# A hybrid attention and HGRN2 block on one core: one more page slot, another block order, and whole rows in the merge

## The chip, the cores and the metric

The kernel runs on 1 core of one Trainium2 chip. The metric is the device time of one execution in microseconds. The engines are named as the profile names them: PE (TensorE), PEld (its weight loads), DVE (VectorE), ACT (ScalarE), POOL (GpSimd) and SP (SyncE, which issues most DMAs). A difference of 0.3% is about what a measurement of this kernel can tell from no change.

## The reference

One layer on 1024 tokens of 1024 features. One input projection `z = rms_norm(x) @ w_in` feeds two branches, everything in float32:

```
q, k, v = qkv of 3 groups x 8 heads of 64;  (window, dilation) = (128,1), (512,4), (2048,16)
o_g = softmax(rms_norm(q) . rms_norm(k) / 8 + bias, in the band) @ v         # per group g
wts = den_g * exp(max_g - max over g)
o_a = sum_g wts_g * o_g / sum_g wts_g                                          # the merge
y_a = (o_a * silu(g_a)) @ w_proj_a
f   = lb + (1 - lb) * sigmoid(z_f);  S_t = diag(f_t) S_(t-1) + (1 - f_t) i_t^T;  o_t = S_t^T q_t
o_b = rms_norm(o_fwd + o_bwd) * silu(g_b);  y_b = o_b @ w_proj_b               # 8 heads, both directions
out = x + (sigmoid(zgate_a) * y_a + sigmoid(zgate_b) * y_b) @ w_out
```

Group g's outputs lie in DRAM by residue classes of its dilation (1, 4 or 16), so a token's three outputs stand at three places of a row.

## The kernel before

**Products in two parts.** Each float32 operand is kept as a high and a low part of type fp32r. A product is three matmuls (high·high, low·high, high·low). The weights come in *pages* of 128x512: loaded into `raw` (or `qraw`), turned into `whi` by ACT, and into `wlo = raw - whi` by DVE or POOL (`split`, line 381). While `b.low` is "dma", `wlo` is made otherwise: ACT writes −`whi` into it, and POOL issues a DMA that adds the page from DRAM. Two rings of RING slots hold the split pages; a slot comes free when PE has used its page (`free_to`).

**Who sets the order.** All instructions are issued by a planner in program order of Python, with an estimate of each engine's time. PE's main stream (projection units, blocks) is written out; between its pieces `tick` (line 274) issues the tasks of the other engines that are due, and `burst` (line 290) the small PE products that are ready. So a change of a ring's size or of an order in one place moves instructions in many. Each engine works through its own list in order. All instructions carry line 60, that of the recording helper, and are told apart by their tiles.

**The stages, in time.**
- 0 to 58 us: h is prepared, and the products `u` of the first value group (pages 0 to 7) run twice over, for the two halves of the tokens (`u_products`, line 985). During the second loop the pages 8 to 15 are split, with `b.low = "dma"`.
- 55 to 148 us: `v` of groups 1 and 2. Tiles `gp`; each sweep reads eight pages, 8 to 15 and then 16 to 23. The first sums `xs` of h for the next stage are made in it.
- 148 to 676 us: 27 *blocks* of seven products each, by Strassen's scheme (`start_quads`, line 413; `run_quads`, line 477). A product is 12 matmuls with one page, and the page is a sum or difference of quarters of the block's weights; these wait in a ring of QRAW tiles of 512 KB, two for each block. The list `blocks` (lines 698 to 701) sets their order: qk (q and k of the attention, with a norm chain of squares, `nss` sums, logarithm and exponential behind each), sg (gates), qb (q of the second branch), gb and ga (gates with silu). Results leave PSUM as `qA`, `qC`, `qE` through `stage` and `spare`.
- 692 to 860 us: the attention, 860 to 921 us: the merge, mixed with the projections of the first HGRN heads.
- 906 to 1234 us: the HGRN heads, 1234 us to the end: the last projections by the seven-product scheme.

**The merge.** `alphas_out` (line 1648) makes the weights of the groups, `alB`. For each of 8 units (four pairs of heads, two halves of the tokens) `merge_load` (line 1649) loads the three group outputs `og` and the gate `gal`, and `spread_al` (line 1684) spreads the weights by three matmuls into three PSUM banks `al`, then multiplies and adds on DVE into `macc`. In halves of a row, group 1's loads have runs of 512 bytes, group 2's of 128 bytes.

**The first HGRN head.** Its transposes `kT` on PE need `sk`, which DVE makes at the end of a chain that begins with the scans `Bc`. On DVE these stand behind the last unit of the merge.

Of the kernel before, what the change touches and what calls it, by code (L numbers as in the profile page):

```python
# [9 lines left out]
F32R = mybir.dt.float32r  # L10
# [3 lines left out]
OP = mybir.AluOpType  # L14
# [4 lines left out]
S = 1024  # L19
# [2 lines left out]
NEG = -1e30  # L22
TABW = 384
WARM = 10
RING = 8
RAWS = 4
LEAD = 4
TAIL, LATE = 4, 4
EARLY = 8
QB = 6  # L30
QRAW, SPARE = 4, 7
RES = (1, 4, 16)
LOWS = ("T2", "T4")
SQ, EA = 2, 6
# [198 lines left out]
class Builder:  # L233
# [179 lines left out]
    def start_quads(self, ring):  # L413
# [238 lines left out]
def hybrid_block(ctx, tc, a, out):  # L652
    b = Builder(ctx, tc, a)
    a_, v_, g_, t_, s_ = b.p.act, b.p.dve, b.p.pool, b.p.pe, b.p.sp
# [19 lines left out]
    def bank(name):  # L674
        t = b.bank.get(name=name)
        b.bank.done(t)
        return t
# [18 lines left out]
    qk = [("qk", g, hv, e) for g in range(3) for hv in range(2) for e in range(2)]  # L696
    sg = [("sg", 0, j) for j in range(0, 8, 2)] + [("sg", 1, j) for j in range(0, TAIL, 2)]
    blocks = []
    for k in range(6):
        blocks += qk[2 * k:2 * k + 1] + sg[k:k + 1] + qk[2 * k + 1:2 * k + 2] + ([("qb", 2 * k - 2)] if 0 < k <= QB // 2 else [])  # L700
    blocks += [("gb", k) for k in range(4)] + [("ga", 0), ("ga", 2)]

    def block_pages(kind, *at):
# [25 lines left out]
    items += [wpa[i] for i in range(8)]  # L729
    b.setup_weights(items, wpool, RING, RAWS)  # L730

# [45 lines left out]
    acc = [v_ring.get() for _ in range(2)]  # L777
# [259 lines left out]
    for j in range(4):  # L1037
        keep_u(j)
    b.low = "dma"
    at = {0: {11: lambda: root(1)}, 3: {5: lambda: root_out(1), 11: lambda: root(0)}, 7: {5: lambda: root_out(0)}}  # L1040
    for d in range(8):
        u_products(1, d, at.get(d, {}))
# [196 lines left out]
    def scaled(g, hv, e, half, z, y2, o, col, count):  # L1239
        R = RES[g]  # L1240
        n = 512 // R
        per = lambda t: t.rearrange("p (r u) -> p r u", r=R) if R > 1 else t
        nat = lambda t: t.rearrange("p (u r) -> p r u", r=R) if R > 1 else t
        v_.tensor_tensor(per(o), nat(y2), nat(z), op=OP.mult)
# [5 lines left out]
        def out():  # L1250
            for i in range(4):
# [333 lines left out]
    mer = {}  # L1585

    def merge_maybe(now=False):
        if mer or not (now or len(stored) == 48) or not att:
            return
        if now:  # L1590
            b.drain()
        b.eager, b.SLACK = False, 0.6
        b.low = "dve"
        psum(3)
        actx.close()
        mer["p"] = mctx.enter_context(tc.tile_pool(name="merge", bufs=1, side="right"))
        mer["sel"] = sel = mer["p"].tile([128, 3, 4, 128], F32R, name="sel")
        mer["x"] = mer["p"].tile([128, 8, 128], F32R, name="mx")
        g_.memset(mer["x"].bitcast(F32), 0.0)
        pick = lambda c: ident[:, c:c + 8].rearrange("p (a j) -> p a j", a=4)[:, :, :, None].to_broadcast([128, 4, 2, 64])  # L1600
        for g in range(3):
            v_.tensor_tensor(sel[:, g].rearrange("p a (j c) -> p a j c", j=2), pick(32 * g), pick(32 * g + 8), op=OP.add)
        mer["og"] = b.ring(mer["p"], "og", 9, [128, 512])
        mer["gal"] = b.ring(mer["p"], "gal", 3, [128, 512])
        mer["acc"] = b.ring(mer["p"], "macc", 2, [128, 512])
        merge_start()

# [38 lines left out]
        b.product(0, [mer["x"]], alphas_out, merge=False, banks=2)  # L1646

    def alphas_out():
        ab = mer["p"].tile([128, S], F32R, name="alB")
        for half in range(2):  # L1650
            p = bank("alT")
            for t in range(4):
                t_.transpose(p[:, 128 * t:128 * t + 128], mer["x"][:, 4 * half + t].bitcast(F32), ident)
            a_.activation(ab[:, 512 * half:512 * half + 512], p, AF.Copy)
        mer["ab"] = ab

    def merge_load(p, half):
        ld = {}

        def og_load(g):  # L1660
            o = mer["og"].get()
            if g == 0:
                s_.dma_start(o, oD[0, p, :, 512 * half:512 * half + 512])
            else:
                R = 4 if g == 1 else 16
                U = S // R
                s_.dma_start(o.rearrange("p (r u) -> p r u", r=R),
                             oD[g, p].rearrange("p (r u) -> p r u", r=R)[:, :, U // 2 * half:U // 2 * half + U // 2])
            ld[g] = o

        def ga_load():
            t = mer["gal"].get()
            s_.dma_start(t, gaD[p, half])
            ld[3] = t

        for g in range(3):
            b.task("sp", [oD], lambda g=g: og_load(g), 1, lambda: mer["og"].soon())
        b.task("sp", [gaD], ga_load, 1, lambda: mer["gal"].soon())
        b.product(4, [], lambda: spread_al(p, half, ld),
                  lambda: len(ld) == 4 and "ab" in mer and b.p.done(mer["ab"]) <= b.p.t["pe"]  # L1680
                  and b.when_all(list(ld.values())) and mer["acc"].soon(),
                  merge=False, banks=3)

    def spread_al(p, half, ld):
# [4 lines left out]
        per = lambda t, g: t.rearrange("p (r u) -> p u r", r=(4, 16)[g - 1])  # L1689
        acc = mer["acc"].get()  # L1690
# [12 lines left out]
    def merge_start():  # L1703
        mer["st"] = st = mer["p"].tile([128, 3, 2, 8, 8], F32, name="nst")
        stats_in()
        a_.activation(st[:, 0], mst[0], AF.Copy)
        b.task("dve", [st], alphas, 3)
        for k in range(8):
            merge_load(k // 2, k % 2)


    def evac_sg(w, j, half):
# [471 lines left out]
    ep, acc, sgr = ectx["ep"], ectx["acc"], ectx["sg"]  # L2184
# [30 lines left out]
    def seven_weights(base, pages, order, along=None, by_dma=()):  # L2215
# [13 lines left out]
        def split(op, i):  # L2229
# [3 lines left out]
            def f():  # L2233
# [346 lines left out]
```

## Time and profile before

| | |
|---|---|
| three runs | 1437.22, 1433.92, 1433.57 us; median 1433.92 |
| profiled execution | 1435.38 us, of which the span of the trace is 1433.6 |
| mean granted clock of PE | 0.995 |
| busy: PE, DVE, ACT, POOL | 1408.3, 918.0, 848.3, 349.5 us |
| DMA | 230.31 MB, mean 161 GB/s |

The span is counted from the first to the last instruction of the profiled execution; times in the text are from its start. A row of a timeline gives the start, the duration, engine, operation, tiles (out<-in) and how many instructions it stands for; in brackets the idle time before it and what ended that. Matmuls overlap: one of 128x512 lasts 0.39 us, and the next can start before it ends. A row of the waits gives what an engine waited for, the total, the number of waits and the longest.

### The profile page before, as it was taken

What the parts mean: (1) busy time and instruction counts of PE and PEld (TensorE: products, weight loads), DVE (VectorE), ACT (ScalarE), POOL (GpSimd) and SP (SyncE); (2) the same over time, 40 slices, a digit from 0 to 9 for tenths busy, and PEclk for the clock granted to TensorE, in tenths of its full rate; (3) what the DMA queues carried; (4) which work ended last, traced back from release to release, by engine and by line L of the source; (5) the groups of instructions that cost most, each with busy time, mean ns of one, the idle gap of its engine ahead of it and who ended that gap; (6) DMA issues with size and microseconds to landing.
All of it is one profiled execution on the core that took longest, in us unless ns stands there. A gap on an engine that the chain in (4) does not pass through costs nothing. (4 is left out here: it accounts for less than half of the span.)

```text
span 1433.6 us, 24071 instructions
## 1 busy us (share of the span) xinstructions
PE 1408.3 (98%) x8506; PEld 1170.7 (82%) x8506; DVE 918.0 (64%) x1890; ACT 848.3 (59%) x1837; POOL 349.5 (24%) x378
## 2 busy tenths in 40 slices
PE   9999999999999999999999999899999999999998
PEld 8778888888888888788778888688888888788887
DVE  6574556666666666542356647978878686358973
ACT  7642656655555565843586642667777684558461
POOL 0100434454433333243141110122123121001011
PEclk9999999999999999999999999999999999999999
DMA  6737566677744434533887239745445443768565
GB/s 225 176 105 212 163 204 160 150 182 174 169 131 118 103 89 98 158 112 117 286 282 254 94 85 273 209 109 126 103 118 126 123 131 87 236 231 220 176 170 143
DMA packets 200804, 230.31 MB, mean 161 GB/s; under 512 B 60531, under 2 KB 125323, under 8 KB 200172
## 3 DMA queue, kind: packets, MB, share of 16 engines
q1 hardware_dynamic: 182876, 193.19, 44.4%
q0 software_dynamic: 16944, 35.40, 13.2%
q8 instruction: 67, 1.10, 0.3%
q14 instruction: 53, 0.43, 0.1%
q10 hardware_dynamic: 864, 0.19, 0.1%
HBM read 168.77 MB, written 81.43 MB: 175 GB/s over the span
## 5 line engine op out<-in xcount | busy, mean ns | idle before, releaser
L60 POOL TENSOR_TENSOR wlo<-qraw,whi 128x512 fp32r<-128x512 f32 x135 | 181.2, 1344 | 390.5 <-ACT whi L60 383.8
L60 ACT ACTIVATE whi<-qraw 128x512 fp32r<-128x512 f32 x189 | 117.7, 626 | 101.6 <-POOL wlo L60 36.8
L60 PE MATMUL gp<-hh,whi 128*128 128x512 f32 x264 | 109.0, 413 | 0.0
L60 DVE TENSOR_TENSOR qraw<-qraw,qraw 128x512 f32<-128x512 f32 x81 | 70.0, 865 | 57.6 <-POOL wlo L60 57.6
L60 PE MATMUL gp<-hh,wlo 128*128 128x512 f32 x264 | 103.6, 392 | 0.0
L60 PE MATMUL gp<-hl,whi 128*128 128x512 f32 x264 | 103.0, 390 | 0.0
L60 ACT ACTIVATE whi<-raw 128x512 fp32r<-128x512 f32 x92 | 57.5, 626 | 75.8 <-DMA raw<-in_w_in_dram 38.3
L60 ACT ACTIVATE as<-as,neg 128x192 f32<-128x192 f32 (+1 forms) x192 | 77.8, 409 | 23.9 <-DVE neg L60 23.9
L60 PE MATMUL qA<-hh,whi 128*128 128x512 f32 x216 | 84.0, 389 | 0.0
L60 PE MATMUL qA<-hl,whi 128*128 128x512 f32 x216 | 84.0, 389 | 0.0
L60 PE MATMUL qA<-hh,wlo 128*128 128x512 f32 x216 | 84.0, 389 | 0.0
L60 PE MATMUL gp<-wlo,hh 128*128 128x512 f32 x192 | 76.0, 396 | 4.0 <-DMA wlo<-in_w_in_dram 3.0
L60 PE MATMUL gp<-whi,hh 128*128 128x512 f32 x192 | 79.6, 415 | 0.0
L60 PE MATMUL gp<-whi,hl 128*128 128x512 f32 x192 | 75.8, 395 | 0.0
L60 POOL COPY mm<-Bc 128x8 f32<-128x8 f32 x64 | 32.5, 543 | 171.6 <-DVE Bc L60 171.6
L60 POOL DMA_DIRECT2D wlo<-in_w_in_dram x36 | 31.1, 864 | 142.1 <-ACT wlo L60 92.3
L60 DVE CUSTOM_DVE_ANT_0 as<-sc,abias 128x192 f32<-128x192 f32 (+1 forms) x192 | 48.4, 308 | 21.3 <-PE sc L60 12.4
L60 PEld LDWEIGHTS gp<-hh,wlo 128*128 128x128 f32 x264 | 49.5, 188 | 10.9
L60 PEld LDWEIGHTS gp<-hh,whi 128*128 128x128 f32 x264 | 49.7, 188 | 8.9
L60 PEld LDWEIGHTS gp<-hl,whi 128*128 128x128 f32 x264 | 49.8, 189 | 8.3
L60 DVE TENSOR_TENSOR wlo<-qraw,whi 128x512 fp32r<-128x512 f32 x54 | 38.4, 711 | 28.2 <-ACT whi L60 28.1
L60 DVE TENSOR_TENSOR ny<-ny,spare 128x512 f32<-128x512 f32 x36 | 55.7, 1549 | 0.0
(316 smaller groups left out, 4123.5 us busy)
## 6 DMA issues: line engine op xcount, KB each, us to landing
raw<-in_w_in_dram SPq DMA_DIRECT2D x84, 256.0 KB, 3.1
qraw<-in_w_in_dram SPq DMA_DIRECT2D x60, 256.0 KB, 4.3
qraw<-in_w_in_dram SPq DMA_DIRECT2D x24, 512.0 KB, 4.4
qkD<-ny SPq DMA_DIRECT2D x192, 64.0 KB, 2.1
wlo<-in_w_in_dram POOLq DMA_DIRECT2D x36, 256.0 KB, 4.4
sg<-sgD SPq DMA_DIRECT2D x32, 256.0 KB, 3.7
eraw<-wsD SPq DMA_DIRECT2D x32, 256.0 KB, 3.1
sgD<-stage SPq DMA_DIRECT2D x26, 256.0 KB, 2.2
```

Of the source, the lines that this page charges most:

```text
L60: got = f(*args, **kw)
```

## The change

The change has three parts:
- RING goes from 8 to 9 slots and QRAW from 4 to 3 tiles, which needs as much memory as before. One more page is split ahead of the second loop of `u_products`.
- The blocks are ordered anew: one qb block goes between the qk blocks, the other two behind all of them and ahead of gb and ga. Before, the three were spread between the qk blocks.
- The merge loads whole rows of a group's output, 12 loads of 512 KB in the order of groups 2, 1, 0, in a ring of 6 tiles of 1024 columns; before, 24 loads of 256 KB in a ring of 9 tiles of 512. The gates' ring goes from 3 to 2, `alB` is written into the tile `mx`, and the product of group 2 is written into its PSUM bank in place of an `og` tile. The rows come free after the second half.

```diff
-RING = 8
+RING = 9
...
-QRAW, SPARE = 4, 7
+QRAW, SPARE = 3, 7
...
-        blocks += qk[2 * k:2 * k + 1] + sg[k:k + 1] + qk[2 * k + 1:2 * k + 2] + ([("qb", 2 * k - 2)] if 0 < k <= QB // 2 else [])
+        blocks += qk[2 * k:2 * k + 1] + sg[k:k + 1] + qk[2 * k + 1:2 * k + 2] + ([("qb", 0)] if k == 2 else [])
+    blocks += [("qb", h) for h in range(2, QB, 2)]
     blocks += [("gb", k) for k in range(4)] + [("ga", 0), ("ga", 2)]
...
     b.low = "dma"
+    b.split_next_page()
     at = {0: {11: lambda: root(1)}, 3: {5: lambda: root_out(1), 11: lambda: root(0)}, 7: {5: lambda: root_out(0)}}
...
-        mer["og"] = b.ring(mer["p"], "og", 9, [128, 512])
-        mer["gal"] = b.ring(mer["p"], "gal", 3, [128, 512])
+        mer["og"] = b.ring(mer["p"], "og", 6, [128, S])
+        mer["gal"] = b.ring(mer["p"], "gal", 2, [128, 512])
...
-        ab = mer["p"].tile([128, S], F32R, name="alB")
+        ab = mer["x"].rearrange("p t h -> p (t h)")
...
+        def og_load(g):
+            rows[g] = mer["og"].get()
+            s_.dma_start(rows[g], oD[g, p])
...
-        for g in range(3):
+        for g in (2, 1, 0):
             b.task("sp", [oD], lambda g=g: og_load(g), 1, lambda: mer["og"].soon())
...
-        v_.tensor_tensor(ld[0], al[0], ld[0], op=OP.mult)
-        v_.tensor_tensor(nat(acc, 1), nat(al[1], 1), per(ld[1], 1), op=OP.mult)
-        v_.tensor_tensor(nat(ld[1], 2), nat(al[2], 2), per(ld[2], 2), op=OP.mult)
-        v_.tensor_tensor(ld[0], ld[0], ld[1], op=OP.add)
-        v_.tensor_tensor(acc, acc, ld[0], op=OP.add)
-        v_.tensor_tensor(acc, acc, ld[3], op=OP.mult)
+        acc, far = mer["acc"].get(), al[2]
+        near = rows[0][:, 512 * half:512 * half + 512]
+        v_.tensor_tensor(near, al[0], near, op=OP.mult)
+        v_.tensor_tensor(nat(acc, 1), nat(al[1], 1), per(1), op=OP.mult)
+        v_.tensor_tensor(nat(far, 2), nat(al[2], 2), per(2), op=OP.mult)
+        v_.tensor_tensor(near, near, far, op=OP.add)
+        v_.tensor_tensor(acc, acc, near, op=OP.add)
+        v_.tensor_tensor(acc, acc, gate, op=OP.mult)
...
-        for g in range(3):
-            mer["og"].done(ld[g])
-        mer["gal"].done(ld[3])
+        mer["gal"].done(gate)
+        if half:
+            for t in rows.values():
+                mer["og"].done(t)
```

What this does to the lists of the engines is shown at three places. PE has the same instructions before and after; between the kernels its list differs in the order of the blocks, of the `al` products and of the HGRN heads' pieces.

The first place is ACT's list at the start of the second loop of `u_products` (lines with - are of before, with + of the changed kernel; `uv` are the results of the first loop, `sq`, `hh` the preparation of h):

```order
 L60 ACTIVATE uv_231<-u_235 128x512
 L60 ACTIVATE uv_232<-u_236 128x512
-L60 ACTIVATE sq_456<-x_140 128x512
+L60 ACTIVATE whi_422<-raw_257 128x512
+L60 ACTIVATE wlo_423<-whi_422 128x512
+L60 ACTIVATE sq_462<-x_140 128x512
 L60 ACTIVATE hh_99<-v_221,nw 128x512
-L60 ACTIVATE whi_461<-raw_257 128x512
-L60 ACTIVATE wlo_462<-whi_461 128x512
```

Page 8 is split ahead of `sq`, and from there on each `whi`, `wlo` of the loop belongs to the page after the one that stood there. POOL's DMA for a page follows its `wlo`.

The second place is ACT's list near the end of the blocks. Before, around the silu (`stage<-stage`) of the first gb block:

```order
L60 ACTIVATE stage_5275<-qE_5255 128x512
L60 ACTIVATE whi_5283<-qraw_5065 128x512
L60 ACT_TABLE_LOAD
L60 ACTIVATE ny_5287<-nss_5277,eps 128x512
L60 ACT_TABLE_LOAD
L60 ACTIVATE ny_5287<-ny_5287 128x512
L60 ACTIVATE ny_5288<-ny_5287 128x512
L60 ACTIVATE stage_5302<-qA_5173 128x512
L60 ACTIVATE whi_5315<-qraw_5072 128x512
```

In the changed kernel, the last norm chain and the first silu:

```order
L60 ACTIVATE ny_5155<-nss_5022,eps 128x512
L60 ACTIVATE ny_5155<-ny_5155 128x512
L60 ACTIVATE ny_5156<-ny_5155 128x512
L60 ACTIVATE stage_5164<-qE_5145 128x512
L60 ACTIVATE whi_5170<-qraw_5101 128x512
L60 ACTIVATE stage_5185<-qA_5074 128x512
L60 ACTIVATE whi_5187<-qraw_4927 128x512
L60 ACTIVATE whi_5210<-qraw_5104 128x512
L60 ACT_TABLE_LOAD
L60 ACTIVATE stage_5089<-stage_5089 128x512
```

The norm chains (`ny<-nss` is the logarithm, `ny<-ny` the exponentials) now all stand ahead of the first silu. ACT has 23 table loads in the whole program, 29 before.

The third place is DVE's list at the end of the merge. Before, the last unit and the first scan:

```order
L60 TENSOR_TENSOR macc_9190<-macc_9190,gal_9006 128x512
L60 TENSOR_TENSOR wlo_9204<-raw_9043,whi_9203 128x512
L60 TENSOR_TENSOR og_9087<-al_9207,og_9087 128x512
L60 TENSOR_TENSOR macc_9213<-al_9208,og_9089 128x512
L60 TENSOR_TENSOR og_9089<-al_9209,og_9091 128x512
L60 TENSOR_TENSOR og_9087<-og_9087,og_9089 128x512
L60 TENSOR_TENSOR macc_9213<-macc_9213,og_9087 128x512
L60 TENSOR_TENSOR macc_9213<-macc_9213,gal_9099 128x512
L60 TENSOR_TENSOR wlo_9236<-raw_9045,whi_9235 128x512
L60 SCALAR_TENSOR_TENSOR Bc_9296<-rst,qr_9286 128x512
```

In the changed kernel:

```order
L60 TENSOR_TENSOR macc_9158<-macc_9158,gal_9079 128x512
L60 TENSOR_TENSOR wlo_9186<-raw_9035,whi_9185 128x512
L60 TENSOR_TENSOR wlo_9204<-raw_9056,whi_9203 128x512
L60 TENSOR_TENSOR og_8984<-al_9207,og_8984 128x512
L60 TENSOR_TENSOR macc_9213<-al_9208,og_8966 128x512
L60 TENSOR_TENSOR al_9209<-al_9209,og_8964 128x512
L60 TENSOR_TENSOR og_8984<-og_8984,al_9209 128x512
L60 TENSOR_TENSOR macc_9213<-macc_9213,gal_9172 128x512
L60 SCALAR_TENSOR_TENSOR Bc_9278<-rst,qr_9268 128x512
```

The third product goes to `al`. Between the unit before and the last one stand two `wlo` in place of one, between the last one and the scan none in place of one. On PE the runs of `gp` matmuls between the eight `al` groups were 6, 42, 24, 36, 24, 36 and 6, with 84 from the last group to the first `kT`; now they are 12, 30, 36, 24, 42, 18 and 24, with 66 to the first `kT`. There `kT` is now four transposes, six `gp` and three more, where it was seven in a row.

More of the change, by code (lines that the diff above doesn't have):

```diff
@@ L1655, in alphas_out, with merge_load, ga_load, spread_al @@
         mer["ab"] = ab
-    def merge_load(p, half):
-        ld = {}
+    def merge_load(p):
+        rows, gate = {}, {}
         def og_load(g):
[L1661 to L1674, printed above, removed]
-        for g in range(3):
-            b.task("sp", [oD], lambda g=g: og_load(g), 1, lambda: mer["og"].soon())
[L1678 to L1684, printed above, removed]
+            rows[g] = mer["og"].get()
+            s_.dma_start(rows[g], oD[g, p])
+        def ga_load(half):
+            gate[half] = mer["gal"].get()
+            s_.dma_start(gate[half], gaD[p, half])
+        for g in (2, 1, 0):
+            b.task("sp", [oD], lambda g=g: og_load(g), 1, lambda: mer["og"].soon())
+        for half in range(2):
+            b.task("sp", [gaD], lambda half=half: ga_load(half), 1, lambda: mer["gal"].soon())
+            b.product(4, [], lambda half=half: spread_al(p, half, rows, gate[half]),
+                      lambda half=half: len(rows) == 3 and half in gate and "ab" in mer
+                      and b.p.done(mer["ab"]) <= b.p.t["pe"] and b.when_all([*rows.values(), gate[half]])
+                      and mer["acc"].soon(),
+                      merge=False, banks=3)
+    def spread_al(p, half, rows, gate):
         al = [bank("al") for _ in range(3)]
@@ L1688, in spread_al, with per @@
         nat = lambda t, g: t.rearrange("p (u r) -> p u r", r=(4, 16)[g - 1])
-        per = lambda t, g: t.rearrange("p (r u) -> p u r", r=(4, 16)[g - 1])
-        acc = mer["acc"].get()
-        v_.tensor_tensor(ld[0], al[0], ld[0], op=OP.mult)
-        v_.tensor_tensor(nat(acc, 1), nat(al[1], 1), per(ld[1], 1), op=OP.mult)
-        v_.tensor_tensor(nat(ld[1], 2), nat(al[2], 2), per(ld[2], 2), op=OP.mult)
-        v_.tensor_tensor(ld[0], ld[0], ld[1], op=OP.add)
-        v_.tensor_tensor(acc, acc, ld[0], op=OP.add)
-        v_.tensor_tensor(acc, acc, ld[3], op=OP.mult)
+        def per(g):
+            U = S // (4, 16)[g - 1]
+            return rows[g].rearrange("p (r u) -> p u r", u=U)[:, U // 2 * half:U // 2 * half + U // 2]
+        acc, far = mer["acc"].get(), al[2]
[6 more added lines that the diff above has]
+        v_.tensor_tensor(acc, acc, gate, op=OP.mult)
         b.task("sp", [acc], lambda: (s_.dma_start(oaD[p, half], acc), mer["acc"].done(acc)), 1)
         mer["out"] = mer.get("out", 0) + 1
-        for g in range(3):
-            mer["og"].done(ld[g])
-        mer["gal"].done(ld[3])
+        mer["gal"].done(gate)
+        if half:
+            for t in rows.values():
+                mer["og"].done(t)
     def merge_start():
@@ L1707, in merge_start @@
         b.task("dve", [st], alphas, 3)
-        for k in range(8):
-            merge_load(k // 2, k % 2)
+        for p in range(4):
+            merge_load(p)
     def evac_sg(w, j, half):
```

## Prediction

> **What bounds the kernel now.** I read first how busy each engine is, then what PE waits for, then the places of those waits in time.
>
> ```profile
> span 1433.6 us, 24071 instructions
> PE   1408.3 (98%) x8506; PEld 1170.7 (82%) x8506; DVE 918.0 (64%) x1890; ACT 848.3 (59%) x1837; POOL 349.5 (24%) x378
> ...
> PE kT L60 <- DVE sk L60: 3.9, 1, 3.9
> PE gp L60 <- DMA wlo<-in_w_in_dram: 3.0, 1, 3.0
> PE qA L60 <- ACT stage L60: 2.7, 1, 2.7
> ...
> PE al L60 <- DVE og L60: 1.8, 1, 1.8
> PE gp L60 <- ACT xh L60: 1.6, 1, 1.6
> ...
> PE oB L60 <- DVE S L60: 1.5, 1, 1.5
> PE gp L60 <- DVE wlo L60: 1.0, 1, 1.0
> ```
>
> PE is busy for 98% of the span, and the change leaves its matmuls as they are. So only two things can move the time by more than a little: PE's few waits (each of the rows is one single gap) and the clock after a gap. A busier or calmer DVE, ACT or DMA counts only where it makes or fills one of those gaps. A view by stretches shows the clock after three of the gaps (the third number from the end of a row; the two behind it are the DMA share and GB/s) and a stretch without any:
>
> ```profile
> 58.30:65.00 6.70, 3.75 (x10) 2.68 (x10) 4.30 (x11) 3.64 (x10) 0.00 (x0) 0.75 0.94 221
> 108.00:585.00 477.00, 477.00 (x2105) 394.84 (x2105) 290.26 (x365) 264.66 (x460) 179.99 (x149) 1.00 0.58 149
> 585.00:592.00 7.00, 4.26 (x20) 3.20 (x19) 2.39 (x4) 6.15 (x8) 0.06 (x1) 1.00 0.60 174
> 932.40:939.00 6.60, 6.41 (x24) 5.78 (x25) 6.57 (x17) 2.51 (x7) 0.38 (x1) 0.53 0.79 204
> ```
>
> After the gaps at 58 and at 928 PE ran at half clock for a while; after the one at 588 it did not. A gap therefore costs its length, and sometimes half as much again or more. From 108 to 585 PE never waits: 2105 matmuls in 477 us, 0.227 us from one start to the next at full clock.
>
> **The change part by part.**
>
> *The extra split and the ninth page slot.* PE stands still for page 15, the last of eight that the first v sweep reads:
>
> ```profile
> 58.34 0.39 PE L60 MATMUL gp<-whi,hh 128*128 128x512 f32 x1
> 61.68 0.80 PE L60 MATMUL gp<-wlo,hh 128*128 128x512 f32 x1 [2.95 <-DMA wlo<-in_w_in_dram]
> ...
> 64.40 0.59 PE L60 MATMUL gp<-wlo,uhi 128*128 128x512 f32 x1
> 64.83 0.40 PE L60 MATMUL gp<-whi,ulo 128*128 128x512 f32 x1
> ```
> ```profile
> 51.75 0.86 POOL L60 DMA_DIRECT2D wlo<-in_w_in_dram  x1 [1.86 <-PE u L60]
> 56.54 0.86 POOL L60 DMA_DIRECT2D wlo<-in_w_in_dram  x1 [3.93 <-ACT wlo L60]
> ```
> ```profile
> DMA to landing us min/median/max: 4.0/4.3/5.1
> ```
>
> From 58.34 to 61.68 are 3.34 us, 3.11 too many; from 61.68 to 64.83 seven matmuls take 3.15 us in place of 1.59, 1.56 too many. Sum 4.7. Now page 8 is split ahead of the loop and each later page moves one place up on ACT, so page 15 takes the place that page 14 had, whose accumulating DMA went out at 51.75. With the slowest landing of the row, 5.1, it is there at 56.9, 1.4 us ahead of the need at 58.3; its own took 61.68 − 56.54 = 5.1. So the whole 4.7 goes. What pays for it is 1.25 us of ACT work ahead of the preparation of h, which has room:
>
> ```profile
> 31.11 0.63 ACT L60 ACTIVATE whi<-raw 128x512 fp32r<-128x512 f32 x1 [0.99 <-PE u L60]
> ...
> 35.39 0.63 ACT L60 ACTIVATE sq<-x 128x512 f32<-128x512 f32 x1 [2.99 <-DVE v L60]
> ```
>
> These two idle times, 4.0 us, cover it. Without that cover h would be 1.25 us late, and PE with it: low end 3.4.
>
> *The next sweep.* PE's wait of 1.0 on DVE's wlo (row above; 1.2 with the restart) is for the low part of one page:
>
> ```profile
> 104.56 2.49 DVE L60 TENSOR_TENSOR xs<-hh,hl 128x512 f32<-128x512 f32 x4
> 106.97 1.89 DVE L60 TENSOR_TENSOR wlo<-raw,whi 128x512 fp32r<-128x512 f32 x3
> ```
>
> The subtraction stands behind four sums on DVE. With nine slots page 16 is split long before, by DMA, so one subtraction fewer (0.6 us) stands in that queue and the late page is one further on, 0.68 us of matmuls later. Between 0 and 1.2; I take half the way, 0.7.
>
> *Block order.* The wait of 2.7 on ACT's stage comes from here:
>
> ```profile
> 586.27 1.28 ACT L60 ACT_TABLE_LOAD   x1
> 587.57 0.69 ACT L60 ACTIVATE ny<-nss,eps 128x512 f32<-128x512 f32 x1
> 588.28 1.28 ACT L60 ACT_TABLE_LOAD   x1
> 589.57 1.29 ACT L60 ACTIVATE ny<-ny 128x512 f32<-128x512 f32 x2
> 590.77 0.58 ACT L60 ACTIVATE stage<-qA 128x512 f32<-128x512 f32 x1
> ```
>
> The evacuation that frees PE's bank stands behind 4.5 us of logarithm, exponential and two table loads, because silu of the gb blocks runs between the norm chains of the last q and k blocks. In the new order two qb blocks, which need no function of a table, stand between; the two last chains run on ACT ahead of the first silu, and six table loads (7.7 us of ACT) are gone. The gap of 2.74 and its restart go: 2.9. The low end is 0, if another evacuation meets the chain; ACT then lacks only 1.3 us twice, not 4.5, so I take 2.9.
>
> *One 512 KB raw tile fewer in the blocks* costs nothing as long as the ring of split pages covers it; this is the first rival, below.
>
> *The merge.* Twelve loads of 512 KB stand for 24 of 256 KB, the bytes are the same. I bound their landing by the weights' loads of both sizes:
>
> ```profile
> qraw<-in_w_in_dram SPq DMA_DIRECT2D x60, 256.0 KB, 4.3
> qraw<-in_w_in_dram SPq DMA_DIRECT2D x24, 512.0 KB, 4.4
> ```
>
> A load of twice the size lands 0.1 us later; three go first, so the first group of al has its rows no later. On DVE a third of the products now writes into PSUM, for which no row exists. The nearest is the same product with PSUM only as input:
>
> ```profile
> L60 DVE TENSOR_TENSOR og<-al,og x16: 683/896/1120, 862.8 to 917.4; 128x512 f32<-128x512 f32 x16
> ```
>
> The strided one is the 1.12 end; I take 1.12, no change. By the ends of the row it is 0.44 shorter, or as much longer, in each of eight groups.
>
> ```profile
> 909.06 0.50 PE L60 MATMUL al<-alB,sel 128*128 128x512 f32 x1 [1.83 <-DVE og L60]
> ```
>
> This wait (2.0 with the restart) comes from an al group six matmuls behind the one before, while DVE still reads the banks. The two groups of the last pair are now 24 apart (5.4 us), those before 18 and more, but for the first two, ahead of which DVE is idle. One group is about 5.0 us on DVE (below), so I book the whole 2.0; low end 0, since the third bank is now held until the third sum (1.4 us longer).
>
> Behind it lies the longest gap:
>
> ```profile
> 928.25 0.39 PE L60 MATMUL gp<-hh,wlo 128*128 128x512 f32 x1
> 932.59 1.73 PE L60 MATMUL kT<-ident,sk 128*128 128x128 f32 x7 [3.95 <-DVE sk L60]
> 934.97 0.63 PE L60 MATMUL gp<-hbh,wlo 128*128 128x512 f32 x1
> ```
> ```profile
> 915.64 0.69 DVE L60 TENSOR_TENSOR og<-al,og 128x512 f32<-128x512 f32 x1
> ...
> 920.01 0.69 DVE L60 TENSOR_TENSOR macc<-macc,gal 128x512 f32<-128x512 f32 x1
> ...
> 921.22 1.22 DVE L60 TENSOR_TENSOR_SCAN Bc<-rst,qr 128x512 f32<-128x512 bf16 x1
> ...
> 931.75 1.16 DVE L60 TENSOR_TENSOR sk<-km,G 128x512 f32<-128x512 f32 x2
> ```
>
> PE is ready for kT at 928.48 and gets it at 932.59: 4.1. Then it runs at half clock up to 938.7; of these 6.1 us half are lost, 3.1. Together 7.2. In the new order PE comes to kT earlier by the 2.0 of the al stall and by six wide matmuls that now follow kT (1.4): at 925.1. Counted back from there, with 66, 24 and 18 matmuls of 0.227 and three of al (0.7) between, the last three al groups end at 910.1, 904.0 and 899.2. DVE begins group 6 at 899, and then has three groups of 5.0 (915.64 to 920.6) and four wlo of 0.6: the first scan starts at 916.4, not 921.22. From the scan to kT the trace has 932.59 − 921.22 = 11.4, so sk is there at 927.8, and a gap of 2.7 stays. Does the clock fall after it? Gaps of 2.95 and 2.74 went either way, so I take half of the 1.6 that the 2.95 one cost, 0.8. The term is 7.2 − 2.7 − 0.8 = 3.7. Ends by the 0.44 of PSUM in each of three groups, 1.3 in all: 7.2 − 1.4 = 5.8 if it is faster and the clock holds, and 7.2 − 4.0 − 3.1 = 0.1 if it is slower and the clock falls as now.
>
> The Trainium skill, page "TensorE: Matmul & The Clock Gate", section "Part 1: The HAM clock gate", says that the clock halves after an idle window of about 3.4 us and that the windows run free of the kernel. By its length a gap of 2.7 would leave the clock alone, and the sum would be 0.8 better; the trace does not bear that out, since the gap of 2.95 halved it. That the outcome hangs on the window's place would fit 2.74 and 2.95.
>
> *Behind the merge.* The other rows: oB's wait of 1.5 (1.7) stems from a state update that DVE reaches late behind a scan; the interleaving there is new, so 0 to 1.7, I take 1.0. xh's wait of 1.6 (1.8) lies at the seam to the last stage; the last onT, on which xh rests, now stands six matmuls earlier there (1.4): 0 to 1.8, I take 1.4. New small gaps have to be expected where the order is new; the smallest of the waits above is 1.0, so I set 2 against the gain for two like it, between 0 and 4.
>
> Sum: 4.7 + 0.7 + 2.9 + 2.0 + 3.7 + 1.0 + 1.4 − 2.0 = 14.4. The profiled execution took 1435.38 (span 1433.6 and 1.8 around it), so it would take 1421.0; the median of the runs lies 1.46 below it, at 1433.92. Forecast for the median: **1419.5**.
>
> **The rivals.**
>
> *The blocks starve (slower).* Three raw tiles hold one block and a half. A block has two tiles of 512 KB and seven products of 12 matmuls, 2.72 us each; the second tile of the next block can only be loaded once the present one gives one up. Load 4.4 (row above), ACT's split 0.63 and the low part on POOL 1.34 make 6.4 us. Nine split pages are 24.5 us of PE work, so if the splitting runs well ahead nothing shows. It decides when the ring at a block's end holds no more than two pages, 5.4 us: then each of 26 seams loses 6.4 − 5.4 = 1.0, 26 in all, and 1419.5 + 26 = 1445.5. Against it speaks that PE now has no gap at all between 108 and 585; for it, that the second tile's slot now comes half a block, 9.5 us, later.
>
> *The stalls of the merge only move.* If DVE's groups take longer with PSUM as their target, or al waits again for a bank, the 2.0 and 3.7 don't come: 1419.5 + 5.7 = 1425.2. For it: DVE has no slack between 899 and kT in my count.
>
> *The head start closes the kT gap further.* With the 5.8 end of that term and no small new gaps (2.0), 1419.5 − 2.1 − 2.0 = 1415.4. For it: the clock held after the 2.74 at 588. Against it: the waits above are spread over all stages, so new places in the order are likely to have some too.
>
> *The early page doesn't arrive earlier*, because the raw load of page 15 or the PE release of its slot is late too, not ACT's place in line: 4.7 stays lost, 1424.2. Against it: what ended the wait ahead of the DMA at 51.75 was PE's use of an older page, so a slot, and of these there is now one more.
>
> **How the numbers follow.** Forecast 0.52, merge stalls only move 0.20, closes further 0.15, page not earlier 0.06, starving blocks 0.07. The likeliest case's own range is 1415 to 1424. With the second and third case the range is 1412 to 1428; the starving blocks and a little at both ends stay outside. What a measurement tells from no change is 0.3%, 4.3 us: faster means under 1429.6, slower over 1438.2. The first four cases all lie below 1429.6, 0.93; of these I put 0.01 over the bound for several terms failing at once. Of the starving case a mild form (half the loss and less, up to 1438) is 0.04, the full one 0.03. So faster 0.92, same 0.05, slower 0.03.
>
> **What would show it.** Right: PE's waits have no wlo DMA at 58 and no half clock at 62; no ACT stage wait near 588 and 23 table loads; PE busy throughout between 108 and 585 as now; the first scan at about 906 to 908 in the new time base (916.4 less the 8.3 gained before it), the kT gap near 2.7; the xh wait under 1. Wrong: waits of PE on whi or wlo at the seams of blocks, an al wait of 2 us or more, or a product into PSUM well over 1.12.

## The result and the profile after

The changed kernel takes 1422.49 us (median of six runs, 1420.24 to 1424.7) beside 1434.73 for the kernel before: a ratio of 0.9911, 95% interval 0.9896 to 0.9926. Faster by 0.9%, where 1.0% was forecast, and 3.0 us slower than the 1419.5 that the prediction gave. The profiled execution took 1421.18 with a span of 1419.4; against the profiled execution of before that is 14.2 less, where the sum had 14.4. The sum came out, but not by its terms: some of them gave more than was booked, a stage that was not in it gave 3.8, and the blocks lost 5.9 us that were hardly in it. That these nearly cancel is luck.

The view of what PE waits for, changed kernel (total, times, longest):

```profile
PE kT L60 <- DVE sk L60: 2.4, 1, 2.4
PE pT L60 <- ACT aos L60: 2.3, 1, 2.3
...
PE qA L60 <- ACT stage L60: 1.3, 1, 1.3
PE nss L60 <- DVE nlo L60: 0.9, 1, 0.9
PE nss L60 <- ACT nhi L60: 0.6, 1, 0.6
PE qA L60 <- ACT spare L60: 0.5, 1, 0.5
...
PE gp L60 <- DVE wlo L60: 0.3, 1, 0.3
...
PE gp L60 <- DVE xl L60: 0.2, 1, 0.2
```

The waits for page 15, al, xh and oB are gone, and that of sc (the scores) at the start of the attention too. This one was the fourth longest of the kernel before, and the prediction had left it out; its gap was followed by half clock, which shows in the clock of its stretch (0.95):

```profile
PE sc L60 <- issue: 2.4, 1, 2.4
692.00:725.00 33.00, 29.84 (x515) 23.80 (x514) 16.51 (x141) 23.52 (x122) 4.59 (x7) 0.95 0.94 316
```

New are the waits of qA and nss, in the blocks, and a longer one of pT in the attention. The changed kernel's stretches by their clock (third number from the end of a row):

```profile
58.30:65.00 6.70, 6.70 (x31) 5.30 (x29) 5.92 (x13) 5.22 (x14) 0.22 (x2) 1.00 0.94 223
108.00:580.00 472.00, 468.15 (x2058) 385.50 (x2057) 310.61 (x364) 263.45 (x460) 189.12 (x149) 1.00 0.58 149
687.00:720.00 33.00, 30.64 (x488) 24.64 (x487) 16.09 (x136) 22.66 (x116) 4.72 (x8) 0.95 0.93 319
895.00:935.00 40.00, 37.23 (x181) 30.71 (x180) 36.46 (x63) 24.46 (x47) 7.79 (x13) 1.00 0.53 157
```

After the kT gap the clock now holds; at the start of the attention it is 0.95 again, now behind pT's gap. In the blocks PE, which was busy for all of 477 us before, is idle for 3.9 of 472.

To have one number for each stage, I add up over all PE instructions of a stretch how much later the next one starts than it could: 0.227 us for a wide matmul, about 0.115 for a small one. It holds the waits, the restarts and the half clock. In us:

| stretch (us) | 0–60 | 60–115 | 115–585 | 585–700 | 700–905 | 905–945 | 945–end | all |
|---|---|---|---|---|---|---|---|---|
| before | 7.4 | 3.8 | 0.1 | 7.4 | 19.6 | 9.4 | 17.5 | 65.3 |
| changed | 4.8 | 1.5 | 5.9 | 0.7 | 21.5 | 4.1 | 12.7 | 51.3 |

The difference of 14.0 is the 14.2 of the spans but for 0.2. Each stage below is read by this loss.

Two of the steps, shown. POOL's DMA for page 15 goes out one place earlier (52.24, it was 56.54; the row at 57.03 is now page 16's):

```profile
52.24 0.86 POOL L60 DMA_DIRECT2D wlo<-in_w_in_dram  x1 [1.86 <-ACT wlo L60]
57.03 0.86 POOL L60 DMA_DIRECT2D wlo<-in_w_in_dram  x1 [3.93 <-PE gp L60]
```

And the first head, with the product into PSUM (columns of the first row: durations in ns, smallest, median, largest):

```profile
L60 DVE TENSOR_TENSOR al<-al,og x8: 1068/1076/1099, 860.7 to 909.1; 128x512 f32<-128x512 f32 x8
```
```profile
912.56 1.23 DVE L60 TENSOR_TENSOR_SCAN Bc<-rst,qr 128x512 f32<-128x512 bf16 x1 [0.22 <-ACT qr L60]
...
922.92 1.15 DVE L60 TENSOR_TENSOR sk<-km,G 128x512 f32<-128x512 f32 x2
```
```profile
923.75 0.63 PE L60 MATMUL kT<-ident,sk 128*128 128x128 f32 x4 [2.44 <-DVE sk L60]
```

The write into PSUM takes 1.08, where 1.12 was assumed; from the scan to kT are 11.2 us, where 11.4 were; the gap is 2.4, where 2.7 was forecast. The scan itself stands at 912.56, and not at 906 to 908 as the prediction's own sign had it: ahead of it the changed kernel had gained 3.9 us (the loss up to 905 fell from 38.3 to 34.4), not the 8.3 that the sign counted with.

### The profile page after: what moved, and what is told of

The parts are those of the page before. It is cut to its first block, busy times and chain, and to the rows that moved or that the text cites. A ratio compares the mean times of both kernels' runs of the same rounds, so it can differ in the third digit from the quotient of the medians.

```text
span 1419.4 us, 24083 instructions
## 1 busy us (share of the span) xinstructions
PE 1404.2 (99%) x8506; PEld 1167.5 (82%) x8506; DVE 932.5 (66%) x1889; ACT 841.3 (59%) x1831; POOL 358.3 (25%) x379
## 4 chain that ended last, share of the span: by engine, by line
PE 80%; DVE 7%; DMA 4%; ACT 4%; issue 4%; SPq 1%; POOL 0%; DVEq 0%; ACTq 0%; POOLq 0%
PE gp L60 28%; PE qA L60 14%; PE qE L60 7%; PE sA L60 6%; PE sE L60 5%; PE qC L60 3%; PE u L60 3%; PE oB L60 3%; DMA qraw<-in_w_in_dram 2%; DVE ny L60 2%; PE sc L60 2%; PE U L60 2%; PE o L60 2%; PE pT L60 2%; DVE qraw L60 1%
## 5 line engine op out<-in xcount | busy, mean ns | idle before, releaser
L60 POOL TENSOR_TENSOR wlo<-qraw,whi 128x512 fp32r<-128x512 f32 x135 | 189.7, 1413 | 377.1 <-ACT whi L60 346.3
L60 DVE TENSOR_TENSOR qraw<-qraw,qraw 128x512 f32<-128x512 f32 x81 | 82.0, 1013 | 46.9 <-DMA qraw<-in_w_in_dram 34.5
L60 DVE CUSTOM_DVE_ANT_0 as<-sc,abias 128x192 f32<-128x192 f32 (+1 forms) x192 | 48.4, 308 | 19.6 <-PE sc L60 18.6
L60 ACT ACTIVATE stage<-gp 128x512 f32<-128x512 f32 x39 | 22.7, 591 | 53.4 <-PE gp L60 42.8
```

The source lines that it names most:

```text
L60: got = f(*args, **kw)
```

## The experiments

The new gaps lie in the blocks. There DVE, which never waited for a load before, now does (idle time until a load of `qraw` landed: us, times, 115 to 585):

```profile
  DMA qraw<-in_w_in_dram: 34.5, 13
```

How such a wait reaches PE, at the worst place of the changed kernel:

```profile
368.76 0.69 DVE L60 TENSOR_TENSOR qraw<-qraw,qraw 128x512 f32<-128x512 f32 x1 [4.12 <-DMA qraw<-in_w_in_dram]
```
```profile
369.49 0.63 ACT L60 ACTIVATE whi<-qraw 128x512 fp32r<-128x512 f32 x1 [6.66 <-DVE qraw L60]
370.03 0.58 ACT L60 ACTIVATE stage<-qE 128x512 f32<-128x512 f32 x1
370.50 0.62 ACT L60 ACTIVATE whi<-qraw 128x512 fp32r<-128x512 f32 x1
371.02 0.59 ACT L60 ACTIVATE stage<-qA 128x512 f32<-128x512 f32 x1
```
```profile
371.66 0.50 PE L60 MATMUL qA<-S2h,whi 128*128 128x512 f32 x1 [1.33 <-ACT stage L60]
```

DVE waits 4.1 for a load before it can form a sum of weights; ACT waits 6.7 for the sum, to split it; behind that split in ACT's list stand two evacuations, and PE waits for the bank that the second one frees. The page that was late is not the one PE wants: the ring still had pages. (Counting ACT's splits against PE's products of 12 matmuls, the splits are 7 pages ahead at this place, and never fewer than 6 before the last pages of the blocks.) So the first theory was that three raw tiles alone make the gaps, the rival (second theory) that the new block order alone does. Four kernels ran together with the kernel before (its median there 1436.79).

**Pages undone.**

```diff
-RING = 9
+RING = 8
-QRAW, SPARE = 3, 7
+QRAW, SPARE = 4, 7
...
     b.low = "dma"
-    b.split_next_page()
```

> The changed kernel with RING 8, QRAW 4 and without the extra split; block order and merge stay as changed. First theory (three raw tiles let the next block's weights land late, ACT stands at a split with evacuations queued behind it, and PE loses 5.9 us between 115 and 585): that loss falls under 1 us, no engine waits for a qraw load in this stretch, and the wait for page 15 with its half clock (4.7) is back: near 1421.5. Second theory (the new block order makes these gaps): the loss stays near 5.9 and the page's wait comes on top, near 1427.

Measured 1421.48 (ratio to before 0.9892, 0.9864 to 0.9920). The loss between 115 and 585 is 0.05, and page 15's wait is back:

```profile
PE gp L60 <- DMA wlo<-in_w_in_dram: 2.3, 1, 2.3
```

So the new order with four tiles makes no gaps. The rival falls.

**Block order undone.**

```diff
-        blocks += ... + ([("qb", 0)] if k == 2 else [])
-    blocks += [("qb", h) for h in range(2, QB, 2)]
+        blocks += ... + ([("qb", 2 * k - 2)] if 0 < k <= QB // 2 else [])
```

> The changed kernel with the block order of before. First theory: waits for qraw loads stay, the loss between 115 and 585 stays 3 to 6 us, and the table wait near 588 (2.9) is back: near 1425. Second theory: the loss between 115 and 585 falls under 1 us, and with the table wait back the time is near 1419.5.

Measured 1417.1 (0.9870, 0.9839 to 0.9900): faster than the changed kernel, not slower. DVE waits for loads as often, but for 28 us rather than 34:

```profile
  DMA qraw<-in_w_in_dram: 28.1, 13
```

The loss between 115 and 585 is 1.0, against 3 to 6 expected. The table wait, expected near 588 with 2.9, comes at 600 with half of that, outside this stretch:

```profile
601.88 0.50 PE L60 MATMUL qC<-hh,whi 128*128 128x512 f32 x1 [1.44 <-ACT spare L60]
```

So the first theory falls as well in its simple form: three tiles make the loads late in either order, but only together with the new order do they cost PE more than 1 to 2 us there. Repeated later on another chip, it was 1418.35 (0.9882, 0.9866 to 0.9899), loss 1.9, with a wait of 1.5 at 600 again:

> The kernel of the second experiment once more (nine slots, three raw tiles, new merge, block order of before), on the same chip as the next three. If the block order is what costs once there are three raw tiles, it stays near 1417 and the loss between 115 and 585 near 1; if the first result was chance, it lies near the changed kernel, 1422.

**Merge undone.** The functions of the merge as before, all else as changed.

> The changed kernel with the merge of before. If my reading of the merge is right, the al wait (2.0), the kT gap of 4 with its half clock (3.1) come back in place of the gap of 2.4: 6 to 7 us slower than the changed kernel, near 1428.5. The rival (the merge part is worth little, its stall only moved): within 2 us of the changed kernel.

Measured 1429.3 (0.9948, 0.9933 to 0.9964), 6.8 more than the changed kernel; as each compares with the kernel before that ran beside it, 4.8 more. Its waits bring back what was expected, and oB's as well:

```profile
PE kT L60 <- DVE sk L60: 3.6, 1, 3.6
...
PE al L60 <- DVE og L60: 1.7, 1, 1.7
...
PE oB L60 <- DVE S L60: 1.5, 1, 1.5
```

**Page 15 by subtraction.** If the ninth slot is only for page 15, and its price is a raw tile, the page can be had otherwise: its low part subtracted by the idle POOL from the raw page, and not added by a DMA of 5 us.

```diff
 (on the kernel with the pages undone)
+    b.low = "pool"
     b.auto()
     for j in range(4):
         scaled_v(j)
```

> RING 8 and QRAW 4 as before, without the extra split, new block order and new merge; in place of the ninth slot page 15's low part is subtracted by POOL and not added by a DMA (POOL 1.3 us in place of 5.1 to landing; it starts near 55.6, the need is at 58.3). First theory: no wait at 58, no loss in the blocks: near 1416.5, faster than the changed kernel by 5 to 6. Second theory: no wait at 58, but the blocks lose 5.9 as in the changed kernel: near 1422.5.

Measured 1418.85 (0.9875, 0.9851 to 0.9899), and 1417.9 (0.9875, 0.9860 to 0.9890) when it ran again:

> The fourth experiment's kernel again, beside the one before: near 1418, loss in 115 to 585 under 0.5. The wait of sc at the start of the attention, which was 2.2 there and 0 in the changed kernel, shows whether it is the run's chance: if so, it may be anything from 0 to 2.6 here.

No wait at 58, losses of 0.03 in the blocks both times. It comes out 1.4 to 2.4 above the 1416.5; sc, which didn't wait in the changed kernel, waits 2.0 in its first and 3.2 in its second profile (shown), which is of that size:

```profile
PE sc L60 <- DMA aq<-qkD: 3.2, 1, 3.2
PE kT L60 <- DVE sk L60: 2.4, 1, 2.4
```

Beside the second of these ran the same kernel in the old block order:

> Four raw tiles, page 15's low part on POOL, new merge, and the block order of before: against the next kernel only the order differs. If the new order is worth its table wait (1.6 to 2.9 us near 590), this is slower than the next by 1.6 to 2.9; if it is worth nothing with four tiles either, the two are within 1 us. In both cases no loss in 115 to 585.

Measured 1421.86 (0.9902, 0.9888 to 0.9917), 4.0 more, with the table wait back at its full size:

```profile
PE qA L60 <- ACT stage L60: 2.6, 1, 2.6
```

This gives a table of two by two, medians in us, all with the new merge:

| | three raw tiles, nine slots | four raw tiles, page 15 on POOL |
|---|---|---|
| old block order | 1417.1 and 1418.35 | 1421.86 |
| new block order | 1422.49 (and 1421.97, below) | 1418.85 and 1417.9 |

By these medians the new order gains 3 to 4 with four tiles and costs 4 to 5 with three. The change joined the two parts that don't go together. Two things limit the figures. The medians come from sets in which the kernel before had 1434.73 to 1436.79, so a difference between sets is sure to no better than about 2. And the loss over all the blocks, 115 to 680, with the table wait at 600 in it, is 5.9 and 5.7 (new order) beside 2.8 and 3.7 (old order) with three tiles, and 0.03 twice beside 4.5 with four: the profiles put 2 to 3 of the 4 to 5 into the blocks, and the rest of it elsewhere. The old order is the better one with three tiles also because its table wait is smaller there (1.4 and 1.5, not 2.6 with half clock behind it); why was not followed.

**Further edits on the best.**

```diff
 (on the kernel with page 15 on POOL)
-        self.split(raw, page=...)
+        self.split(raw, "pool" if self.low == "dve" and k in (17, 19, 21, 23) else None, page=...)
...
-                      lambda: left["in"] < 3 and att["s"].soon(2), banks=4 if g < 2 else 2)
+                      lambda: left["in"] < 3 and att["s"].soon(2), banks=4 if g < 2 else 2,
+                      after=max(b.p.done(x) for x in (KT[k], QT[k], BIAS[k])) + (6.0 if k == (2, 0) else 0.0))
```

> The kernel before, with two further edits: the low parts of pages 17, 19, 21 and 23 on the idle POOL, and the first scores of the attention planned 15 matmuls (3.4 us) later in PE's list. If PE's wait for DVE's low parts near 101 (1.2) and the wait of sc for its loads (0 to 2.6, and half clock behind it 1.6) go: 1 to 5 us faster than the kernel before, near 1415. If the delay only moves work that then lacks as filler later in the attention: no faster.

Measured 1425.06 (0.9927, 0.9912 to 0.9941), 7 slower than without the edits. sc's wait is gone, but these are longer or new:

```profile
PE kT L60 <- DVE sk L60: 3.0, 1, 3.0
PE al L60 <- DVE og L60: 2.9, 2, 2.2
PE gp L60 <- DVE wlo L60: 1.8, 1, 1.8
```

The wait of the second sweep grew (1.0 to 1.8, with half clock behind it: loss 5.0 in 60 to 115, not 2.2). DVE was slower there: beside each of POOL's four subtractions one of its instructions took about 1.1 us longer. In the kernel without the edits the same two instructions take 0.68 each:

```profile
94.79 1.79 DVE L60 TENSOR_TENSOR S0l<-xs,S0h 128x512 fp32r<-128x512 f32 x1
96.50 1.78 DVE L60 TENSOR_TENSOR wlo<-raw,whi 128x512 fp32r<-128x512 f32 x1
```

And with the scores moved, the planner's list for attention and merge came out anew, with an al wait like that of before. How the delay of the scores leads to that was not followed, and the two edits did not run apart.

The last four ran together (before: 1435.9).

**The changed kernel again.**

> The changed kernel once more, on the chip of the next three. The gaps in the blocks (5.9 us between 115 and 585) stay as they were if they come from its order and its three raw tiles, and the time is near 1422. The wait of sc at the start of the attention (0 in its first profile, 2.0 to 3.4 in others) may come up here if it is the run's chance.

Measured 1421.97 (0.9900, 0.9882 to 0.9918). The loss between 115 and 585 is 5.7, with gaps at the same six places. sc again doesn't wait; pT's wait is 0.6 in place of 2.3, and another of 1.9 stands near it. So the gaps in the blocks belong to the kernel. sc's wait may as well, but two profiles of each kernel are few (0 and 0 here, 2.0 and 3.2 with page 15 on POOL, 0.9 and 0 in the old order with three tiles). The later waits of the attention move around from run to run.

**Nine slots and four tiles.** The memory is taken from the results' ring.

```diff
-QRAW, SPARE = 3, 7
+QRAW, SPARE = 4, 5
```

> The changed kernel with four raw tiles and still nine page slots; the memory comes from the ring of results that wait for their norm chain, 5 tiles in place of 7. If the late loads make the gaps, the loss between 115 and 585 falls under 1 and the time is near 1416.5, below the kernel with page 15 on POOL, since the ninth slot also saves 0.7 in the second sweep and about 1 at the seam to the last stage. If five tiles are too few, evacuations wait for a free tile, and the loss in the blocks is as large as now or larger.

Measured 1422.4 (0.9904, 0.9888 to 0.9920). DVE has no wait for loads between 115 and 580, but the loss there is 7.4, all of another kind:

```profile
PE qA L60 <- ACT spare L60: 4.3, 8, 1.1
```

Evacuations into `spare` wait for a free tile. (This is read from the lists: at 272 the evacuation starts as DVE ends the first of two sums that read `spare`; the view itself names PE as what released it.) Whichever of the two rings gives up memory, something waits in the blocks.

**Three tiles alone.**

```diff
-QRAW, SPARE = 4, 7
+QRAW, SPARE = 3, 7
```

> The kernel before, with three raw tiles as the only edit. If three tiles cost only together with the new order: DVE waits for loads about 13 times as in the changed kernel, but PE's loss between 115 and 585 stays under 2 us and the time within 2 us of before. If they cost by themselves: 4 to 6 us slower than before.

Measured 1434.23 (0.9989, 0.9977 to 1.0001): no change that the runs can tell. DVE waits as often as expected, for 2 us each, the loss between 115 and 585 is 0.6, and in place of the table wait of 2.7 PE waits 0.8 near 588 and 1.7 at 610 for `stage`:

```profile
  DMA qraw<-in_w_in_dram: 22.6, 12
```

**The merge alone.** Only the merge's functions as changed, all else as before.

> The kernel before, with the new merge as the only edit. If the merge's gain is its own, as the undone merge showed (6.8 us between the medians): the al wait of 1.8 is gone, the kT gap falls from 3.9 to about 2.4 without half clock behind it, and oB's wait of 1.5 is gone: 6 to 8 us faster than before. If it needed the other parts: less than 4.

Measured 1424.86 (0.9920, 0.9898 to 0.9942), 11 less than before by the medians and 8.9 by the spans of the two profiles, a little more than expected. al and oB wait no more, and kT's gap fell to 2.4 as expected; page 15, sc and the table wait stand as they did:

```profile
PE gp L60 <- DMA wlo<-in_w_in_dram: 2.9, 1, 2.9
PE sc L60 <- issue: 2.9, 1, 2.9
PE qA L60 <- ACT stage L60: 2.6, 1, 2.6
PE kT L60 <- DVE sk L60: 2.4, 1, 2.4
```

That the clock holds behind the kT gap did not come:

```profile
922.00:940.00 18.00, 15.57 (x82) 12.94 (x81) 14.09 (x35) 11.09 (x24) 5.70 (x9) 0.91 0.71 198
```

The merge is the larger part of what the change gains, and it does so by itself.

**What separates hidden from shown.** In each kernel with three tiles I set DVE's waits for a load beside PE's gaps. In the changed kernel three waits are longer than 3.6 us, at 248 (3.8), 369 (4.1) and 466 (5.1); at 4, 1 and 12 us behind them lie PE's gaps (0.65, 1.5, and a run of 0.8, 1.2 and 0.4). The repeat has the same (4.2, 3.9, 5.1). In the old order the one longest, 3.7, has a gap of 0.6 behind it, and with three tiles alone none is over 3.0 and no gap of 0.5 follows. One small gap, near 291, has no such wait ahead. So in these kernels the length of the wait, at about 3.6 us, goes with the gaps. The way from wait to gap is as above at 248 and 369, where PE stands at a bank (2.1 of the 5.9). At 466 it is another: DVE's step of the norm chain stands behind the late sum in its list and runs at 469.31 (462.67 with four tiles), and PE waits for the two parts `nhi` and `nlo` that the `nss` sums need. That these gaps, 12 us later, come from the wait is read from the lists only. Why the new order makes three of the waits longer was not settled.

## Why the prediction was right, and where not

Point by point, in us of loss:

| step | booked | came |
|---|---|---|
| page 15 and its half clock | 4.7 | 4.7 (3.1 in 0–60, 1.6 in 60–115) |
| start of the program | not in the sum | −0.5 (0–60) |
| the second sweep | 0.7 | 0.7 (1.2 to 0.5) |
| table wait at 588 | 2.9 | 2.9 |
| al, kT and the clock | 2.0 + 3.7 | 5.3 (905–945) |
| oB and xh | 1.0 + 1.4 | 4.8 (945–end), of it 1.7 + 1.8 |
| new gaps | −2.0 | −5.9 in the blocks, −1.9 in the attention |
| start of the attention | not in the sum | 3.8 (585–700 without the table wait) |

**Page 15, the sweep and the tables** went as worked out. The wait and the half clock at 62 are gone and undoing the pages brings the wait back. The 0.5 lost ahead of it lies at the start of the program: the clock rises to full speed at 6.79 us in the profile of before and at 7.82 in that of the changed kernel, and the first four matmuls of `u` take 1.58 and 2.05. The 0.7 of the sweep was half of a bound, and it came: the wait is 0.3 to 0.4 in the kernels with nine slots and 1.0 in those with eight (1.8 with the further edits). The qA wait near 588 is gone with the new order. With the old one it is back at 2.6 if there are four raw tiles, and smaller if there are three (above).

**The kT gap** was right step by step once the smaller gain ahead of it is taken off: scan, chain and gap to 0.3. The wait of `U` behind it (0.4 to 0.5) counts in 945–end before and in 905–945 now; without it the two rows of the table read 5.8 and 4.4. Of the clock I had booked half of a loss, and it held. The Trainium skill, page "TensorE: Matmul & The Clock Gate", section "Part 1: The HAM clock gate", gives an idle window of about 3.4 us as what halves the clock, on windows that run free of the kernel. That the windows run free and that they last 3.4 us agrees with the runs (last section); that a window must be idle throughout does not, for 2.0 us of idle time in one window were enough. The kernel with page 15 on POOL shows both, in its two profiles (first and second run of the same kernel; each first row holds the wait of sc, each second one that of kT, 2.4 both times):

```profile
682.00:692.00 10.00, 7.98 (x118) 6.42 (x117) 4.34 (x53) 3.55 (x18) 0.00 (x0) 0.83 0.88 292
914.00:924.00 10.00, 7.56 (x35) 6.16 (x34) 9.90 (x24) 7.41 (x18) 3.66 (x6) 0.83 0.90 250
```
```profile
682.00:692.00 10.00, 6.78 (x120) 5.51 (x119) 3.04 (x37) 2.36 (x15) 0.00 (x0) 1.00 0.73 227
914.00:924.00 10.00, 7.24 (x39) 5.72 (x38) 9.86 (x22) 8.52 (x20) 3.85 (x6) 1.00 0.96 269
```

After gaps of 2.0 and 2.4 the clock was at 0.83 in the first, after 3.2 and 2.4 at 1.00 in the second. In the first run each gap lies within one window, 2.02 and 2.44; in the second the border of two windows divides each, 1.67 and 1.55, 0.91 and 1.53. So an expected value was the right way to book it: where the borders lie differs from run to run, and that the clock held here is luck.

**oB and xh** were undersized: 2.4 booked, 3.5 by their own waits; the rest of the 4.8 is the wait of `U` and small gaps that were not followed. oB's wait is gone with the new merge alone and back with the old, so it hangs on the merge's order, of which I had only a guess between 0 and 1.7. xh's fell whole, and by two parts of the change, where the prediction had only the six matmuls: it is 1.6 before, 0.7 to 1.0 with the new merge and eight slots, 0.5 with nine slots and the old merge, and gone with both.

**The blocks** are the step that failed, in the term for new gaps and in the first rival. The rival had the cause, a raw tile fewer, and the wrong place where it decides. I let it bite only when the ring of split pages runs down to two, and at every seam; that never happened, for PE did not wait for a page. It bites in the lists of ACT and DVE. At 248 and 369 a split that waits for data holds up the evacuations behind it on ACT, and PE stands at a bank; at 466, as far as the lists show, the late sum holds up a norm chain on DVE. Of 13 late loads these three are followed by gaps. And it needed the other part of the change: with the old order the same three tiles cost 0.6 to 1.9 between 115 and 585. The two edits were costed one by one, each at its own place, so nothing in the working could show that one makes the other dear.

**The start of the attention** was taken as unchanged, and it gave 3.8. Its instructions are the same. The first scores start 10.4 us after the issue of `aq` in the kernel before and 8.2 after it in the changed one; that it is `aq` they wait for, the view says in the kernel with page 15 on POOL (above), not in the one before. The half clock behind sc's gap is in the 3.8, and the one behind pT's gap in the −1.9 of the attention, so in part the loss has moved. Which other transfers make the difference stayed open, and so did whether it is chance: none of the edits separates the kernels with the wait from those without.

**The median** came out 3.0 above the forecast although the profiled execution came out only 0.2 above its own (1421.18 beside 1421.0). The forecast took the profiled execution to lie 1.46 above the median, as it did by the three runs of before; in the changed kernel it lies 1.31 below. Six of its runs spread over 4.5 us, 1420.2 to 1424.7, and the profiled one was among the faster. By the medians of six runs each the gain is 12.2, not 14.2. The attention's waits (pT's 2.3 in one profile, 0.6 and another of 1.9 in the next) and the clock behind the gaps are of that size.

## What to carry to other kernels

A transfer that comes late costs nothing as long as only its own consumer waits; look at what stands behind that consumer in its engine's list, for it is the work queued there, here the evacuations, that stops the bottleneck. Parts of a change that draw on the same memory or the same slack have to be costed together, and run as two by two: here three tiles alone changed nothing that the runs can tell and the new order was good with four, and the order cost 4 to 5 us by the medians where there were three. And before a buffer is bought with another one, ask what it is for: one page on an idle engine did the ninth slot's work at page 15, and that kernel (1417.9 and 1418.85) beat the changed one as did the changed one with the old order (1417.1 and 1418.35).

## What the runs showed of the hardware that was not expected

- Gaps of 2.0, 2.3, 2.45 and 2.95 us were followed by half clock, gaps of 2.74, 2.9 (page 15 with the merge alone) and 3.2 were not, and the kT gap of 2.4 went either way in two runs of one kernel. Between 2 and 3.2 us the length of a gap doesn't say whether the clock falls, and half clock alone moves a run by 1.6.
- The place of the gap says it. Each trace records when the granted clock changes, and within a trace the changes lie whole multiples of 3.413 us apart: in the kernel before, half clock begins at 61.40, 696.28 and 931.80, with 186 and 69 such windows between, and lasts one window, or two behind the gap of 3.95. I laid these windows over PE's idle time in all fourteen profiles, without the start and the last 6 us. Behind each of the 20 windows with 2.0 us of idle time or more, the next one ran at half clock; behind none with 1.75 or less did half clock begin; the six between 1.81 and 1.93 went three and three.
- DVE writes a strided product into PSUM in 1.08 us, as fast as into SBUF (1.05 to 1.12).
- Low parts by POOL took 1.4 to 1.85 us each in the second sweep, and single DVE instructions beside them 1.8 in place of 0.7. In the blocks the low parts took 1.3 by the median, but a quarter of the changed kernel's 144 took over 1.4.
